# A two-layer hybrid mixer block: gate input evicted first, output weights loaded in order of use, last columns in two banks, and a new table of waiting times

## The chip, the cores and the metric

The kernel runs on one core of a Trainium2 chip. The metric is the time of one execution on the device in microseconds (us). A measurement is the median of several runs; beside them stands one execution recorded by the hardware profiler, from which all rows below come. The engines are TensorE (PE; its weight loads are PEld), VectorE (DVE), ScalarE (ACT), GpSimd (POOL) and SyncE (SP, which here only issues DMAs).

## The reference

Two layers act on 256 context and 256 latent tokens of width 1024. Each layer normalises its input, modulates it by a conditioning vector, runs four token mixers in parallel on it (multi-head latent attention, neighbourhood attention, Hyena long convolution, gated linear attention), gates each branch with SiLU, projects it to 1024, merges the four with sigmoid gates, applies one output projection, normalises and adds the residual:

```python
h = modulate(rms_norm(x, pre_g), shift, scale)
ys = [mla(h), na(h), hyena(h), gla(h)]                   # each (tokens, 512)
ys = [y * silu(in_proj(h, z)) for y, z in zip(ys, Z)]
merged = 0.25 * sum(sigmoid(in_proj(h, merge[i])) * (ys[i] @ w_branch[i]) for i in range(4))
x = x + gate * rms_norm(merged @ w_out, post_g)
```

Context tokens read only context; latents read both. Only the latent stream of the last layer is the output, so layer 1 computes the context only where latents need it. All inputs are float32.

## The kernel before

Tokens lie in four tiles of 128, as two pairs: pair 1 the context, pair 0 the latents; channels lie in chunks of 512. A float32 product is made of three matmuls of a rounded type (`mm3`): high part by high part, high by low, low by high, of which one takes 128 rows by up to 512 columns. A weight comes in a piece of 512 KB (`piece`, L426): SP loads it into one of three `raw` buffers, ACT rounds each half to `wh` (L439), DVE subtracts to get `wl` (L380). Both go into one of eight slots of the weight pool, or, for a piece marked spare, into tiles `w` of a larger pool. A `raw` buffer is free when both halves are subtracted; a slot is free when the last matmul has read it. PSUM is split into three pools: two banks for main products (pj, br, wo), four for helpers (pa, pc, lat, scores), two for transposes and small products (pt, glrp, ht, mt).

The order of PE's instructions is written out by the program, not found by a scheduler. A dozen generators (main thread, latents, attention, GLA, Hyena, filters, conditioning) yield; `drive` (L312) keeps a clock which each matmul and transpose advances by a modelled cost (`mm`, `tr`), and takes the first ready task by priority. A generator that yields `self.wait(name)` is ready again when the clock has moved on by the number in the table `WAIT` (one per layer, in us of PE work); the main thread (priority 5) fills what is between. So a larger number puts more main matmuls in front of a group. The other engines' instruction order, and which buffer a tile gets, are settled by a scheduler at build time from this program; every engine then executes its own list in order.

The change touches: `latents` (L897), which transposes the normalised low-rank rows of one token tile (lat into one PSUM bank, glrp, the gate's low-rank input, into another of a two-bank pool) and evicts them (cqT, ckvT, rotT, glrT); `project_out` (L1382), which loads the eight pieces of w_out, makes wo for each token tile in two halves of 512 columns, squares (ACT), multiplies by the gate (DVE), takes `rstd` (DVE, POOL), adds the residual (DVE) and stores; `merge_one` and `turn_merged` stand before it (br: branch product, gt: gated part on DVE, mt, mh, ml: the merged sum transposed and split).

Of the kernel before, what the change touches and what calls it, by code (L numbers as in the profile page):

```python
# [10 lines left out]
F32R = mybir.dt.float32r  # L11
U8 = mybir.dt.uint8
AF = mybir.ActivationFunctionType
# [112 lines left out]
def _layout(x, c, ctx, c_ctx, ada_w, ada_b, pre_g, post_g, w_in, mla_q_norm, mla_w_uq, mla_kv_norm, mla_w_ukv, na_rpb,  # L126
# [81 lines left out]
    "ada_at0": (3.68, 7.47),  # L208
    "ada_at1": (6.0, 11.0),
    "ada_at2": (15.0, 17.0),  # L210
    "ada_at3": (17.5, 19.5),
    "ada_sum": (1.34, 0),
    "ada_load": (7.75, 9.57),
    "ada_gap": (4.19, 8.22),
    "norm": (3.44, 4.0),
    "norm_turn": (6.66, 5.25),
    "norm_ab": (0.16, 0.69),
    "norm_step": (0.65, 0.52),
    "filt_in": (3.1, 4.0),
    "filt_sin1": (6.0, 15.54),  # L220
    "filt_sin2": (6.0, 4.8),
    "filt_w3": (4.0, 4.49),
    "filt_step": (0.48, 0.82),
    "filt_sum": (10.0, 11.8),
    "filt_norm": (7.2, 15.6),
    "filt_dft": (0.3, 0.5),
    "filt_out": (1.82, 4.04),
    "probs": (5.63, 6.08),
    "probs2": (7.2, 7.7),
    "probs_out": (1.36, 0.94),  # L230
    "values_out": (1.14, 5.3),
    "latent_in": (2.81, 1.5),
    "latents": (10.0, 11.79),
    "latents_out": (5.62, 0.49),
    "mla_keys": (1.6, 1.78),
    "mla_v": (0.32, 0),
    "mla_k": (0.8, 2.25),
    "mla_q": (0.15, 0),
    "mla_q_out": (1.7, 1.04),
    "na_in": (2.87, 0.97),  # L240
    "hy_turn": (1.49, 4.79),
    "hy_turn_step": (0.35, 0.5),
    "hy_turn_out": (0.5, 0.67),
    "hy_dft": (1.57, 2.98),
    "hy_product": (12.59, 11.95),
    "hy_mid": (0.35, 0.81),
    "hy_out_step": (0.72, 0),
    "hy_order": (6.38, 0.9),
    "hy_out": (1.3, 1.0),
    "gla_in": (2.65, 0.67),  # L250
    "gla_logit": (1.02, 0.1),
    "gla_decay": (7.1, 2.9),
    "gla_dir": (6.31, 4.0),
    "gla_norm": (14.0, 4.73),
    "gla_turn": (0.03, 0.45),
    "gla_out": (1.66, 1.98),
    "gla_keys": (6.49, 5.03),
    "gla_kT": (0.9, 1.07),
    "gla_at": (0.5, 0.5),
    "gla_scores": (5.09, 7.57),  # L260
    "gla_o": (2.0, 1.05),
    "merged": (4.6, 3.55),
    "merged_step": (0.48, 0),
    "merged_out": (0.82, 1.24),
    "norm_first": (3.27, 8.0),
}


class Task:
    def __init__(self, gen, prio, ready):  # L270
# [1325 lines left out]
```

## Time and profile before

| | |
|---|---|
| median of 3 runs | 1361.12 us (1359.09 to 1361.54) |
| profiled execution, its own time | 1358.52 us |
| its span, first to last instruction | 1356.7 us |
| mean granted PE clock | 0.993 |
| busy: PE, DVE, ACT, POOL | 1299.6, 889.4, 607.1, 318.3 us |
| DMA | 171.08 MB, mean 126 GB/s |

The busy time of an engine is the time in which it has an instruction running. In a timeline a row stands for one instruction or several alike in a row (xN); the bracket at its end is the idle time of the engine before it, and what ended it. Waits group these idle times by who ended them. A granted clock of 1.00 is TensorE's full speed of 2.4 GHz, 0.50 is 1.2 GHz; a stretch's number is the mean over it.

### The profile page before, as it was taken

Reading aid. Unit: us, or ns where it says so; the run is one execution under the profiler, and the core shown is the slowest. Engines: PE = TensorE matmul, PEld = TensorE weight load, DVE = VectorE, ACT = ScalarE, POOL = GpSimd, SP = SyncE. Lnnn points to the kernel's source line nnn. Section 1 sums busy time; section 2 is a strip of 40 time slices with the busy share of each in tenths; the row PEclk is TensorE's granted clock in tenths of the full one; section 3 lists DMA queues with packets and bytes.
Section 4 is the critical chain, followed back from the end, with each engine's and each line's share of the span. In section 5 each row is a group of like instructions: output and inputs, shape, how many; then the busy total and the mean of one; then the engine's idle time right before and its main releaser. Section 6 shows DMA issues by size and latency. Waiting matters only on the chain. (4 is left out here: it accounts for less than half of the span.)

```text
span 1356.7 us, 20161 instructions
## 1 busy us (share of the span) xinstructions
PE 1299.6 (96%) x7444; PEld 1023.7 (75%) x7444; DVE 889.4 (66%) x1660; ACT 607.1 (45%) x1282; POOL 318.3 (23%) x408
## 2 busy tenths in 40 slices
PE   5999999999999999999999999899999999999996
PEld 3877677777777776778767778787767899678875
DVE  5778666575143547676476597887579776768864
ACT  4655556233233332222344444575475456434552
POOL 2332213333030101124111123342123421121210
PEclk9999999999999999999999999999999999999999
DMA  9521222233243433324422352432135366434361
GB/s 350 214 93 40 93 70 77 94 110 109 94 155 124 145 120 108 124 94 139 142 77 80 114 192 85 138 106 99 48 115 158 115 211 212 156 101 153 118 208 63
DMA packets 55507, 171.08 MB, mean 126 GB/s; under 512 B 7470, under 2 KB 10128, under 8 KB 55408
## 3 DMA queue, kind: packets, MB, share of 16 engines
q1 hardware_dynamic: 49056, 153.31, 34.1%
q0 software_dynamic: 5440, 16.16, 3.8%
q8 instruction: 59, 0.97, 0.3%
q10 hardware_dynamic: 912, 0.31, 0.1%
q14 instruction: 40, 0.33, 0.1%
HBM read 163.45 MB, written 6.31 MB: 125 GB/s over the span
## 5 line engine op out<-in xcount | busy, mean ns | idle before, releaser
L380 DVE TENSOR_TENSOR wl<-raw,wh 128x512 fp32r<-128x512 f32 (+1 forms) x416 | 299.0, 740 | 191.2 <-ACT wh L439 186.3
L439 ACT CAST wh<-raw 128x512 fp32r<-128x512 f32 (+1 forms) x416 | 248.5, 617 | 285.1 <-DMA raw<-in_w_in 156.2
L390 PE MATMUL pc<-hh,wh 128*128 128x256 f32 (+1 forms) x688 | 239.8, 349 | 2.1 <-DVE kr L906 1.5
L390 PE MATMUL pc<-hh,wl 128*128 128x256 f32 (+1 forms) x688 | 229.8, 334 | 0.0
L390 PE MATMUL pc<-hl,wh 128*128 128x256 f32 (+1 forms) x688 | 229.3, 333 | 0.0
L390 PE MATMUL pj<-wh,hh 128*128 128x512 f32 x512 | 212.7, 415 | 1.5 <-ACT wh L439 0.8
L390 PE MATMUL pj<-wl,hh 128*128 128x512 f32 x512 | 200.6, 392 | 0.8 <-DVE wl L380 0.6
L390 PE MATMUL pj<-wh,hl 128*128 128x512 f32 x512 | 200.3, 391 | 0.0
L390 PEld LDWEIGHTS pc<-hh,wh 128*128 128x128 f32 x688 | 131.2, 191 | 25.6 <-issue 10.9
L390 PEld LDWEIGHTS pc<-hl,wh 128*128 128x128 f32 x688 | 131.2, 191 | 13.8 <-issue 2.4
L390 PEld LDWEIGHTS pc<-hh,wl 128*128 128x128 f32 x688 | 130.8, 190 | 13.3
L390 PEld LDWEIGHTS pj<-wh,hh 128*128 128x128 f32 x512 | 96.2, 188 | 32.3 <-issue 12.5
L390 PEld LDWEIGHTS pj<-wl,hh 128*128 128x128 f32 x512 | 96.4, 188 | 23.2 <-DVE wl L380 3.6
L390 PEld LDWEIGHTS pj<-wh,hl 128*128 128x128 f32 x512 | 96.1, 188 | 20.9
L380 POOL TENSOR_TENSOR gl<-y,gh 128x256 fp32r<-128x256 f32 (+1 forms) x44 | 36.6, 839 | 302.7 <-ACT gh L422 287.3
L826 ACT ACTIVATE p<-sc,mx 128x512 f32<-128x512 f32 (+1 forms) x96 | 59.0, 616 | 57.9 <-DVE mx L824 54.0
L390 PE MATMUL br<-wh,gh 128*128 128x512 f32 x192 | 77.2, 402 | 2.3 <-DVE gt L383 2.3
L390 PE MATMUL br<-wl,gh 128*128 128x512 f32 x192 | 75.1, 391 | 1.6 <-DVE wl L380 1.6
L390 PE MATMUL br<-wh,gl 128*128 128x512 f32 x192 | 74.9, 390 | 0.0
L1347 ACT ACTIVATE gt<-pj 128x512 f32<-128x512 f32 x48 | 28.6, 596 | 93.2 <-PE pj L390 93.0
L824 DVE TENSOR_REDUCE mx<-sc 128x1 f32<-128x512 f32 (+1 forms) x96 | 55.1, 591 | 11.5 <-PE sc L390 10.6
L377 POOL TENSOR_TENSOR merged<-merged,gt 128x512 f32<-128x512 f32 x24 | 33.1, 1385 | 83.8 <-DVE gt L383 83.8
(286 smaller groups left out, 2213.9 us busy)
## 6 DMA issues: line engine op xcount, KB each, us to landing
raw<-in_w_in SPq DMA_DIRECT2D x160, 512.0 KB, 3.6
adaw<-in_ada_w SPq DMA_DIRECT2D x36, 512.0 KB, 3.8
raw<-in_w_branch SPq DMA_DIRECT2D x32, 512.0 KB, 3.6
raw<-in_w_out SPq DMA_DIRECT2D x16, 512.0 KB, 4.4
adaw<-in_ada_w SPq DMA_DIRECT2D x24, 256.0 KB, 5.2
H<-filt POOLq DMA_DIRECT2D x16, 256.0 KB, 4.0
nab<-in_na_bias POOLq DMA_DIRECT2D x16, 256.0 KB, 3.0
raw<-in_w_in SPq DMA_DIRECT2D x8, 448.0 KB, 4.2
```

The lines of the kernel that those rows point to most:

```text
L377: eng.tensor_tensor(out=out, in0=a, in1=b, op=ALU.add)
L380: eng.tensor_tensor(out=out, in0=a, in1=b, op=ALU.subtract)
L390: self.nc.tensor.matmul(out, lhsT, rhs, start=start, stop=stop, skip_group_check=skip)
L439: nc.scalar.copy(hi, raw[:, sl])
L824: nc.vector.tensor_reduce(out=mx, in_=ps[h][:, :nk], axis=AX.X, op=ALU.max, negate=True)
L826: nc.scalar.activation(p[h][:, :nk], ps[h][:, :nk], AF.Exp, bias=mx, scale=1.0, accum_out=sm)
L1347: self.nc.scalar.activation(gates[s, t], ps, AF.Tanh, scale=0.5)
```

## The change

Four edits. In `latents`, the transpose of the gate input and its eviction glrT come ahead of the evictions of the latents. In `project_out`, the pieces of w_out are loaded as they are used (half 1's first two, half 0's first two, then the rest) instead of all of half 1 first; as before, half 1's pieces are spare tiles and half 0's take weight slots. For the last token tile of layer 1, half 0's 512 columns are made in two PSUM banks of 256 columns (`last_half`), with square, product and sum of each part after its matmuls; the end of the chain is spread over DVE, ACT and POOL. The modelled cost of a matmul gets 32 columns more, and 0.1 where the shape of the PE tile changes; the table of waits is scaled by about 1.06, and some entries are set anew.

```diff
-    "ada_gap": (4.19, 8.22),
-    "norm": (3.44, 4.0),
-    "norm_turn": (6.66, 5.25),
+    "ada_gap": (1.65, 8.71),
+    "norm": (4.8, 3.77),
+    "norm_turn": (5.59, 5.57),
...
-    "hy_mid": (0.35, 0.81),
+    "hy_mid": (0.37, 0),
...
-    "gla_turn": (0.03, 0.45),
+    "gla_turn": (1.89, 0.48),
...
-    "gla_kT": (0.9, 1.07),
-    "gla_at": (0.5, 0.5),
-    "gla_scores": (5.09, 7.57),
+    "gla_kT": (0.63, 1.13),
+    "gla_at": (0, 0.53),
+    "gla_scores": (4.1, 8.02),
...
-            cost = cols / 2400 if rhs.dtype == F32R else 4 * max(cols, 64) / 2400
+            cost = (cols + 32) / 2400 if rhs.dtype == F32R else 4 * max(cols, 64) / 2400
+        mode = (64 if lhsT.shape[0] <= 64 else 128, 32 if out.shape[0] <= 32 else 64 if out.shape[0] <= 64 else 128)
+        if mode != self.mode:
+            self.mode = mode
+            cost += 0.1
...
         parts = [(b, self.cqT[b], self.pp(l, "q_norm", b)) for b in range(2) if full] + [(2, self.ckvT, self.pp(l, "kv_norm"))]
+        pg = self.ps(self.pt, "glrp")
+        self.tr(pg[:96, 0:P], kr[:, 128:224])
+        nc.scalar.copy(self.glrT[:96, sl], pg[:96, 0:P])
         for b, dst, g in parts:
             nc.scalar.activation(dst[0][:, sl], pp[:, b, :], AF.Copy, scale=g)
...
-        pg = self.ps(self.pt, "glrp")
-        self.tr(pg[:96, 0:P], kr[:, 128:224])
-        nc.scalar.copy(self.glrT[:96, sl], pg[:96, 0:P])
...
-        ws = {half: self.rows([self.piece(d["w_out"][l, half, j], 2, 512, half == 1) for j in range(4)]) for half in (1, 0)}
+        order = [(half, j) for step in (0, 1) for half in (1, 0) for j in (2 * step, 2 * step + 1)]
+        got = {(half, j): self.piece(d["w_out"][l, half, j], 2, 512, half == 1) for half, j in order}
+        ws = {half: self.rows([got[half, j] for j in range(4)]) for half in (1, 0)}
...
+                        if last and half == 0:
+                            break
...
+                if last:
+                    yield from self.last_half(ps[0], [t[:, :, P : 2 * P] for t in mT[s]], ws[0], ss, gate[s][0], [o[half][:, 1, :] for half in (0, 1)], x)
+                    continue
...
+    def last_half(self, ps, m, w, ss, gate, y, x):
+        nc = self.nc
+        pair = [ps, self.ps(self.pmm, "wo")]
+        parts, junk = self.t(2, "lss"), self.T("junk")
+        sl = [slice(0, 256), slice(256, 512)]
+        sq = lambda g: nc.scalar.activation(junk[:, sl[g]], pair[g][:, 0:256], AF.Square, scale=D ** -0.5, accum_out=parts[:, g : g + 1])
+        times = lambda g: self.mul(nc.vector, y[0][:, sl[g]], pair[g][:, 0:256], gate[:, sl[g]])
+        for g in range(2):
+            for kt in range(KT):
+                self.mm3(pair[g][:, 0:256], [t[:, kt, :] for t in m], [t[:, sl[g]] for t in w(kt)], kt == 0, kt == KT - 1)
+                yield 0
+            sq(g)
+            if g == 0:
+                times(0)
+                self.add(nc.vector, ss[:, 0:1], ss[:, 1:2], parts[:, 0:1])
+        r, v = self.t(1, "rstd"), self.t(1, "ms")
+        self.ts(v, parts[:, 1:2], ss[:, 0:1], ALU.add, EPS, ALU.add)
+        nc.gpsimd.tensor_tensor(out=r, in0=v, in1=self.mhalf[:, :1], op=ALU.pow)
+        times(1)
+        nc.scalar.activation(y[0][:, sl[0]], y[0][:, sl[0]], AF.Copy, scale=r)
+        self.add(nc.gpsimd, y[0][:, sl[0]], y[0][:, sl[0]], x[0][:, sl[0]])
+        self.stt(y[1], y[1], r, x[1], ALU.mult, ALU.add)
+        nc.sync.dma_start(self.out[1][:, 512:1024], y[1])
+        nc.sync.dma_start(self.out[1][:, 0:256], y[0][:, sl[0]])
+        self.stt(y[0][:, sl[1]], y[0][:, sl[1]], r, x[0][:, sl[1]], ALU.mult, ALU.add)
+        nc.sync.dma_start(self.out[1][:, 256:512], y[0][:, sl[1]])
```

Line numbers of the rows below are those of each kernel, so the same call has another number after the change. First place: ACT, the latents of layer 0. lat_837, lat_852, lat_867 are the PSUM banks of the first three token tiles, glrp their gate inputs. Before, from the last copy of the second tile on:

```order
L935 COPY rotT_258<-lat_852 128x128
L934 ACTIVATE cqT_252<-lat_867,par_122 128x128
L934 ACTIVATE cqT_254<-lat_867,par_122 128x128
L934 ACTIVATE ckvT_256<-lat_867,par_122 128x128
L940 CAST glrT_259<-glrp_849 96x128
L940 CAST glrT_259<-glrp_864 96x128
...
L940 CAST glrT_259<-glrp_879 96x128
```

After, from the first gate input on:

```order
L943 CAST glrT_259<-glrp_842 96x128
L945 ACTIVATE cqT_252<-lat_837,par_122 128x128
L945 ACTIVATE cqT_254<-lat_837,par_122 128x128
L945 ACTIVATE ckvT_256<-lat_837,par_122 128x128
L946 COPY rotT_258<-lat_837 128x128
L945 ACTIVATE cqT_252<-lat_852,par_122 128x128
L945 ACTIVATE cqT_254<-lat_852,par_122 128x128
L943 CAST glrT_259<-glrp_857 96x128
L945 ACTIVATE ckvT_256<-lat_852,par_122 128x128
...
L943 CAST glrT_259<-glrp_872 96x128
```

The first gate input now stands ahead of all latents, the second behind two of the second tile's, and the third behind two of the third tile's.

Second place: the end of layer 0, where w_out's pieces come in. raw_7506 and raw_7516 are the first two pieces in either order; br_7356, br_7371 and br_7386 are branch products, gt what DVE makes of them. DVE before:

```order
L380 TENSOR_TENSOR w_7513<-raw_7506,w_7512 128x512
L383 SCALAR_TENSOR_TENSOR gt_6950<-gt_6950,br_7356 128x512
L380 TENSOR_TENSOR w_7519<-raw_7516,w_7518 128x512
L377 TENSOR_TENSOR merged_2506<-merged_2506,gt_6950 128x512
L380 TENSOR_TENSOR w_7523<-raw_7516,w_7522 128x512
L383 SCALAR_TENSOR_TENSOR gt_6991<-gt_6991,br_7371 128x512
L377 TENSOR_TENSOR merged_2506<-merged_2506,gt_6991 128x512
```

DVE after:

```order
L381 TENSOR_TENSOR w_7513<-raw_7506,w_7512 128x512
L381 TENSOR_TENSOR w_7519<-raw_7516,w_7518 128x512
L381 TENSOR_TENSOR w_7523<-raw_7516,w_7522 128x512
L384 SCALAR_TENSOR_TENSOR gt_6924<-gt_6924,br_7356 128x512
L378 TENSOR_TENSOR merged_2512<-merged_2512,gt_6924 128x512
L384 SCALAR_TENSOR_TENSOR gt_6977<-gt_6977,br_7371 128x512
L378 TENSOR_TENSOR merged_2512<-merged_2512,gt_6977 128x512
```

Both halves of the second piece now stand ahead of the first gt, which frees the PSUM bank of br_7356.

ACT at the same place, before, where raw_7526 and raw_7536 are the third and fourth pieces, and mh the split of the transposed merge:

```order
L439 CAST w_7528<-raw_7526 128x512
L439 CAST w_7532<-raw_7526 128x512
L439 CAST w_7538<-raw_7536 128x512
L439 CAST w_7542<-raw_7536 128x512
L1377 ACTIVATE mh_7420<-mt_7422 128x4x128
L1377 ACTIVATE mh_7420<-mt_7432 128x4x128
L439 CAST wh_7548<-raw_7546 128x512
```

ACT after, where raw_7526 and raw_7536 hold half 0's first pieces (cast to wh_7528 to wh_7542), raw_7546 and raw_7556 half 1's last:

```order
L447 CAST w_7548<-raw_7546 128x512
L447 CAST w_7552<-raw_7546 128x512
L1385 ACTIVATE mh_7420<-mt_7422 128x4x128
L447 CAST w_7558<-raw_7556 128x512
L1385 ACTIVATE mh_7420<-mt_7432 128x4x128
L447 CAST w_7562<-raw_7556 128x512
L447 CAST wh_7528<-raw_7526 128x512
L447 CAST wh_7532<-raw_7526 128x512
```

The third and fourth pieces by SP's order are cast behind the fifth and sixth, and the second mh stands behind a cast of the sixth.

Third place: PE at the start of layer 1. ht are the transposes of the second token pair (one row of four stands for each), pa products of the pair that was normalised first, f the filters, pc a product that takes its bank from the same pool as pa. Before:

```order
L390 MATMUL pa_8127<-wh_8102,hl_7883 128x224
...
L404 MATMUL ht_8264<-ident,xn_8180 128x128
...
L390 MATMUL f_2042_8314<-w3h_8134,a_1890_7695 128x512
...
L390 MATMUL pc_8339<-hh_7882,wh_8331 128x256
...
L404 MATMUL ht_8346<-ident,xn_8180 128x128
...
L390 MATMUL f_2063_8358<-w3h_8134,a_1890_7695 128x512
...
L390 MATMUL pc_8339<-hh_7882,wh_8331 128x256
...
L404 MATMUL ht_8371<-ident,xn_8181 128x128
```

After:

```order
L409 MATMUL ht_8252<-ident,xn_8168 128x128
...
L391 MATMUL pa_8127<-wh_8122,hh_7888 128x224
...
L409 MATMUL ht_8274<-ident,xn_8168 128x128
...
L391 MATMUL f_2044_8324<-w3h_8134,a_1888_7688 128x512
...
L409 MATMUL ht_8331<-ident,xn_8169 128x128
...
L391 MATMUL pc_8359<-hh_7888,wh_8351 128x256
...
L409 MATMUL ht_8366<-ident,xn_8169 128x128
```

The first transposes stand ahead of the last products pa, and three of four ahead of the first pc.

## Rows read from the trace of the kernel before

**Rows 1.** The profile page, its first line and the first row of busy time.

```profile
span 1356.7 us, 20161 instructions
...
PE 1299.6 (96%) x7444; PEld 1023.7 (75%) x7444; DVE 889.4 (66%) x1660; ACT 607.1 (45%) x1282; POOL 318.3 (23%) x408
```

**Rows 2.** Timeline, 72-75 us: start, duration, engine, line, operation, tiles, idle before.

```profile
72.42 0.47 ACT L940 CAST glrT<-glrp 96x128 fp32r<-96x128 f32 x2
...
72.77 0.32 PE L404 MATMUL glrp<-ident,kr 128*96 128x128 f32 x1 [1.89 <-ACT glrT L940]
...
74.32 0.63 PE L390 MATMUL pc<-hh,wh 128*128 128x512 f32 x1
```

**Rows 3.** Busy by stretch: length, PE, PEld, DVE, ACT, POOL, PEclk, DMA share, GB/s.

```profile
69.00:73.00 4.00, 2.12 (x18) 1.78 (x17) 4.00 (x8) 3.51 (x16) 1.81 (x2) 1.00 0.37 85
...
73.00:78.00 5.00, 5.00 (x19) 4.08 (x18) 3.13 (x10) 2.93 (x11) 0.00 (x0) 0.66 0.23 89
...
893.20:896.60 3.40, 3.40 (x17) 3.21 (x16) 1.89 (x7) 2.18 (x7) 1.00 (x3) 0.50 0.09 34
```

**Rows 4.** Waits of PE in 100 to 190 us: total, times, longest.

```profile
PE q L390 <- ACT wuq L422: 1.7, 2, 1.1
...
PE pt L404 <- DVE p L387: 1.3, 2, 0.7
```

**Rows 5.** Timeline of the first GLA, 262 to 295 us, PE and DVE.

```profile
262.91 0.73 PE L390 MATMUL atp<-qp,ktl 64*64 64x64 f32 x26
...
267.20 1.85 DVE L1314 COPY_PREDICATED at<-causal,atp 64x256 f32<-64x256 uint8 x4 [0.22 <-POOL at L1304]
...
290.67 1.29 DVE L380 TENSOR_TENSOR wl<-raw,wh 128x512 fp32r<-128x512 f32 x2 [3.44 <-ACT wh L439]
...
294.44 0.63 PE L404 MATMUL ktp<-ident,ktl 128*128 128x128 f32 x4 [1.46 <-DVE ut L383]
```

**Rows 6.** Timeline at the end of layer 0, DVE and PE.

```profile
786.70 1.76 DVE L380 TENSOR_TENSOR w<-raw,w 128x512 fp32r<-128x512 f32 x1
...
788.98 0.68 DVE L380 TENSOR_TENSOR w<-raw,w 128x512 fp32r<-128x512 f32 x1
...
789.11 0.50 PE L390 MATMUL br<-wh,gh 128*128 128x512 f32 x1 [1.94 <-DVE gt L383]
...
801.06 0.39 PE L390 MATMUL br<-wh,gl 128*128 128x512 f32 x1
```

**Rows 7.** The page, DMA issues: tiles, queue, count, KB each, median us to landing.

```profile
raw<-in_w_out SPq DMA_DIRECT2D x16, 512.0 KB, 4.4
```

**Rows 8.** Timeline of PE at the start of layer 1.

```profile
881.69 0.36 PE L390 MATMUL pc<-hh,wh 128*128 128x256 f32 x1 [1.51 <-DVE kr L906]
...
887.82 0.36 PE L390 MATMUL pa<-wh,hl 128*128 128x192 f32 x1 [0.61 <-DVE hl L380]
...
892.52 0.36 PE L390 MATMUL pa<-wh,hl 128*128 128x192 f32 x1 [1.04 <-DVE hl L380]
```

**Rows 9.** Waits of PE, whole span: total, times, longest.

```profile
PE pj L390 <- DVE wl L380: 0.6, 3, 0.2
```

**Rows 10.** Timeline: 256-column matmuls at 883 us, then the end of the program.

```profile
883.49 0.28 PE L390 MATMUL pc<-hl,wh 128*128 128x256 f32 x1
...
883.61 0.28 PE L390 MATMUL pc<-hh,wl 128*128 128x256 f32 x1
...
1346.67 0.39 PE L390 MATMUL wo<-wl,mh 128*128 128x512 f32 x1
...
1346.90 0.39 PE L390 MATMUL wo<-wh,ml 128*128 128x512 f32 x1
...
1347.32 0.60 ACT L1409 ACTIVATE junk<-wo 128x512 f32<-128x512 f32 x1 [4.75 <-PE wo L390]
...
1348.04 0.69 DVE L374 TENSOR_TENSOR o<-wo,gate 128x512 f32<-128x512 f32 x1 [4.75 <-ACT junk L1409]
...
1348.93 0.56 POOL L411 TENSOR_TENSOR rstd<-ms,mhalf 128x1 f32<-128x1 f32 x1 [10.30 <-DVE ms L387]
```

More of the change, by code (lines that the diff above doesn't have):

```diff
@@ L207 @@
 WAIT = {
[L208 to L213, printed above, removed]
-    "ada_gap": (4.19, 8.22),
-    "norm": (3.44, 4.0),
-    "norm_turn": (6.66, 5.25),
[L217 to L241, printed above, removed]
@@ L259 @@
-    "gla_at": (0.5, 0.5),
-    "gla_scores": (5.09, 7.57),
[L261 to L265, printed above, removed]
+    "ada_at0": (3.9, 7.92),
+    "ada_at1": (6.36, 9.93),
+    "ada_at2": (15.9, 18.02),
+    "ada_at3": (18.55, 20.67),
+    "ada_sum": (0.71, 0.0),
+    "ada_load": (8.21, 10.14),
+    "ada_gap": (1.65, 8.71),
+    "norm": (4.8, 3.77),
+    "norm_turn": (5.59, 5.57),
+    "norm_ab": (0.17, 0.73),
@@ new lines @@
+    "norm_step": (0.69, 0.26),
+    "filt_in": (3.17, 3.48),
+    "filt_sin1": (6.36, 11.83),
+    "filt_sin2": (6.94, 5.09),
+    "filt_w3": (4.24, 3.41),
+    "filt_step": (0.51, 0.87),
+    "filt_sum": (10.6, 11.74),
+    "filt_norm": (7.63, 16.54),
+    "filt_dft": (0.32, 0.53),
+    "filt_out": (1.93, 4.28),
+    "probs": (5.97, 6.44),
+    "probs2": (7.63, 8.16),
+    "probs_out": (1.44, 1.0),
+    "values_out": (1.21, 5.62),
+    "latent_in": (2.98, 1.59),
+    "latents": (10.6, 12.72),
@@ new lines @@
+    "latents_out": (5.96, 0.52),
+    "mla_keys": (1.7, 1.89),
+    "mla_v": (0.67, 0.0),
+    "mla_k": (0.85, 2.39),
+    "mla_q": (0.16, 0.0),
+    "mla_q_out": (1.8, 1.1),
+    "na_in": (4.17, 1.7),
+    "hy_turn": (1.58, 5.08),
+    "hy_turn_step": (0.35, 0.53),
+    "hy_turn_out": (0.53, 0.71),
+    "hy_dft": (1.66, 3.16),
+    "hy_product": (13.35, 12.67),
+    "hy_mid": (0.37, 0),
+    "hy_out_step": (0.76, 0.0),
+    "hy_order": (6.76, 0.95),
+    "hy_out": (1.38, 1.06),
+    "gla_in": (2.81, 0.71),
@@ L266 @@
+    "gla_logit": (1.08, 0.11),
+    "gla_decay": (7.53, 3.07),
+    "gla_dir": (6.69, 4.24),
+    "gla_norm": (14.84, 5.01),
+    "gla_turn": (1.89, 0.48),
+    "gla_out": (1.76, 2.1),
+    "gla_keys": (6.88, 5.98),
+    "gla_kT": (0.63, 1.13),
+    "gla_at": (0, 0.53),
+    "gla_scores": (4.1, 8.02),
+    "gla_o": (2.12, 1.11),
+    "merged": (4.88, 3.76),
+    "merged_step": (0.51, 0.0),
+    "merged_out": (0.87, 1.31),
+    "norm_first": (3.47, 8.48),
 }
@@ L298, in __init__ @@
         self.clock = 0.0
+        self.mode = (128, 128)
         self.l = 0
@@ L404, in tr @@
         self.nc.tensor.transpose(out, in_, self.ident)
+        if self.mode != (128, 128):
+            self.mode = (128, 128)
+            self.clock += 0.1
         self.clock += 0.107
@@ L1394, in project_out @@
                     ps = {half: self.ps(self.pmm, "wo") for half in (1, 0)}
+                last = i == 1 and l == DEPTH - 1 and s == streams[-1]
                 for step in (0, 1) if i == 0 else ((0, 1),):
```

14 lines of the change are left out of this document (removed).

## The prediction

> **What bounds the kernel now.** I read the page first, then the waits of PE, then the timeline where those waits sit, and the clock by stretch. The page says that PE decides: it is busy for 1299.6 of 1356.7 us, and no other engine is above 66% [rows 1]. So the time can move in three ways only: the number and length of matmuls, the idle time of PE, and the clock that PE is granted. The change leaves the matmuls as they are but for one place (24 of 512 columns become 48 of 256). What it can win or lose is therefore waits, some 57 us of idle PE in all (1356.7 less 1299.6), scattered in pieces of 0.3 to 2 us, and the half-rate stretches that follow some of them. A new table of waiting times shifts hundreds of PE groups by a few matmuls; only where a group stood next to a wait does that matter. I went through these places in order of time, comparing the order of the engines before and after.
>
> **The change, part by part.** Terms are microseconds on the profiled execution, which took 1358.5 us by its own time (span 1356.7 and 1.8 around it); that is 2.6 below the median of the three runs, 1361.1, so the sum is carried over to the median as a difference.
>
> *Gate input first, layer 0.* The transpose into glrp at 72.77 has waited 1.89 us for ACT's glrT at 72.42 [rows 2]: the two PSUM buffers of that pool come free only when ACT has got through the latents of three tiles. In 69 to 73 PE works 2.12 of 4 us, and then in 73 to 78 the granted clock is 0.66 on average although PE is busy throughout [rows 3]: 0.34 of 5 us, 1.7 us, is lost at the lower level (the matmul at 74.32 takes 0.63 us [rows 2]; it comes down to 1.2 GHz). After the change glrT of the first tile leaves ACT before any latent, and that of the second after seven copies instead of twelve. ACT is 3.51 of 4 us busy there [rows 3], so the transposes of the fourth tile still find a copy to wait for; I leave 0.8 of the 1.89 and take 1.1 plus the whole 1.7: **-2.8**. From both sides: the wait can move whole to the next latent's buffer (0), or go with the clock fall (-3.6).
>
> *Start and MLA of layer 0.* In 100 to 190 us PE waits 1.7 us for the query weights and 1.3 for p [rows 4]. After the change three groups that wait there have three to six main matmuls more ahead of them; the query weights stand where they stood. I take back most of the 1.3: **-1.2**, with 0 to -3 for the other waits of this stage; the first 70 us are dealt out anew (their first matmuls, transposes and conditioning weights change places), which I put at nothing, 1.5 either way.
>
> *First GLA of layer 0.* The masked scores of the second pair of chunks end on PE at 263.64 and their four copies on DVE at 269.05, 5.4 us later [rows 5]. Before, PE came back for them well after that. The new table (gla_at 0 instead of 0.5, gla_scores 4.10 instead of 5.09) has PE back after 15 main matmuls and one conditioning group, some 4.2 us: a new wait of 1.2. The transposes at 294.44 already wait 1.46, since DVE sat 3.44 us for the weight behind 290.67 and the state chain stood behind it [rows 5]. After the change the same two weight halves stand inside the chain, and their transfer waits for a conditioning group that is now only 6 us of PE ahead of it; 0.6 longer. **+1.8**, from 0 (copies find DVE free) to +4 (the third and fourth pair wait too).
>
> *Order of w_out, end of layer 0.* The matmul at 789.11 waits 1.94 us for gt on DVE, which stood behind one subtraction of 1.76 us [rows 6]. In the new order two more subtractions of w_out, 7518's and 7522's, stand ahead of this gt: 0.60 each at the pace of the 0.68 instruction at 788.98, so +1.2. Further: the third and fourth transfers are now the first pieces of half 0. These are not spare tiles; they take the slots of the branch weights, which PE reads until the last matmul of that branch's pair at 801.06 [rows 6]. So two of the three raw buffers hold pieces that can't be cast, and the next three pieces go through one: each needs 4.4 us to land [rows 7] and then two casts and two subtractions, about 0.65 each, before the next. By ACT's order the second cast of the transposed merge (mh) now stands behind such a cast, and by DVE's order ml and the gt that frees the next branch's PSUM stand behind its subtraction. Counting from the end of 7522's subtraction near 790, 4.4 + 2.6 + 4.4 + 0.6 puts that cast at 802 and the gt near 804, where PE wants its buffer 1.2 later than before, near 803: +1.2; and the first output matmul, which needs the following gt, +1.0. **+3.4** in all, from +1.2 (only the first) to +8 (subtractions at 1.76 and a clock fall behind the waits). In layer 1 no matmul waits for a w_out weight, and mh and ml keep their place behind the same number of casts: 0.
>
> *Start of layer 1.* PE waits 1.51 at 881.69, 0.61 at 887.82, 1.04 at 892.52 [rows 8], and from 893.2 the clock is 0.50 for 3.4 us [rows 3], which costs 1.7. The new order puts three of the four transposes of the second token pair ahead of the first products pc, and DVE and ACT take their modulation up to ten places earlier, so hl, by the count of instructions that no longer stand ahead of it, is ready 1.2 to 2.3 us sooner. The wait at 881.69 is for kr, which stays behind the same weight and now behind one more modulation: it stays. Of the 1.65 of hl I take 1.3, and the 1.7 of the clock: **-3.0**; -0.9 if the clock falls all the same and kr comes later, -4.2 if the waits between go too.
>
> *Rest of layer 1.* In the hyena stage three or four subtractions of weights stand one product further back on DVE, just where PE now waits 0.6 in three pieces for wl [rows 9]: **+0.5**, -1 to +1.5.
>
> *Last 512 columns.* Matmuls of 256 columns start 0.12 us apart (883.49, 883.61), those of 512 columns 0.23 (1346.67, 1346.90) [rows 10]: 48 by 0.118 less 24 by 0.23 is +0.2 with rounding. Behind them, ACT's square covers 256 columns, about 0.2 less than 0.60, and the last matmul itself is 0.1 shorter; above all ms no longer stands behind the 0.6 of DVE's product at 1348.04 [rows 10]. That makes -0.9. What follows rstd stays: instead of two instructions on DVE (twice 0.7, as the product at 1348.04) it is a scale on ACT and then an addition on POOL, after which the last transfer is issued, also about 1.4; I count nothing for the halved transfer. **-0.6**, from -1.4 to +0.3.
> The Trainium skill, TensorEngine Tiling (Array Packing), section Instruction Overhead, speaks against this edit: each matmul carries some 60 cycles of its own. By that, 24 more matmuls at 2.4 GHz would cost 0.6 us instead of 0.2, an estimate from that page, and this term would be -0.2. The trace doesn't agree: two starts of 0.118 against one of 0.23 leave next to nothing for the second instruction.
>
> Sum: -2.8 - 1.2 + 1.8 + 3.4 - 3.0 + 0.5 - 0.6 = **-1.9**: 1356.6 for the profiled execution, 1359.2 at the median.
>
> **The rivals.** *A: the loads stay hidden.* If DVE and ACT reach the moved gt, mh and copies in time, because transfers land in less than 4.4 us or an engine works off its queue while PE is on main matmuls, the +1.8 and +3.4 vanish: -7.1, 1354.0. For it: the view of PE's waits has one only between 780 and 815 us, the 1.94 at 789.11, so there is slack; against it: engines take their instructions in order, and the order is fixed. *B, slower: w_out blocks the end of layer 0.* The two subtractions run at 1.76, as the one before them does, instead of 0.60: +2.3. The chain of single-buffer loads is 1 us later for it, and four waits close together bring the clock down once, 1.7. That is +5.0 on the sum, +3.1 in all: 1364.2. It decides from 4.6 us of loss there beyond the 3.4, for only then is the sum slower by more than a measurement tells apart. *C: waits move only.* Without the clock gains of 1.7 at 73 and 893 us (the level falls after other waits) and with the loss in the GLA halved: -1.9 + 3.4 - 0.9 = +0.6, 1361.7. *D: the table doesn't act*, its shifts all landing between waits; then w_out, latents and tail alone are left, -2.8 + 3.4 - 0.6 = 0.0, 1361.1.
>
> **How the numbers follow.** Forecast 0.45, A 0.20, B 0.20, C and D together 0.15. A measurement of this kernel tells about 0.2%, 2.7 us, from no change. The forecast at -1.9 with its own range of 1356 to 1362.5 gives 0.20 faster, 0.23 no change, 0.02 slower; A all faster; B 0.19 slower; C and D 0.11 no change, 0.02 each side. Together, with rounding, 0.42, 0.35 and 0.23. The half-widths of the terms (1.8, 2.3, 2, 3.4, 1.7, 1.3, 0.9), taken as independent, make 5.5, and the medians of three runs some 1.2 more; so 1351.5 to 1366.
>
> **What would show it.** In the profile after: PE's glrp wait of 1.89 under 1 and a clock of 1.00 in 73 to 78; go waiting 1 us or more for DVE's copies near 265; br's wait for gt at 789 growing to 3, and two new waits before the first output matmul; the waits on hl near 887 and 892 gone and no half-rate stretch behind them; in the last 10 us ms ahead of DVE's product. The prediction is wrong where br waits no longer than before (A), where a clock fall near 790 to 805 appears (B), or where the half-rate stretches stay (C).

## The result, and the profile after

The changed kernel takes 1369.41 us (median of 5 runs, 1365.16 to 1371.32); the kernel before, beside it, 1359.09 (5 runs). The ratio is 1.0064, 95% interval 1.0046 to 1.0081. The forecast was 1359.2 with a range to 1366.0: it is outside, on the slow side. The profiled execution took 1371.32 us, 12.8 more than that of before (the medians are 10.3 apart).

The page of the changed kernel, its first line and its first row of busy time, answers to [rows 1]:

```profile
span 1369.5 us, 20212 instructions
...
PE 1308.9 (96%) x7468; PEld 1031.1 (75%) x7468; DVE 889.3 (65%) x1662; ACT 605.3 (44%) x1285; POOL 325.3 (24%) x409
```

PE is busy 9.3 us longer with the same work (24 matmuls more, of half the size), so most of the loss is not idle time as such. It is time at the lower clock: by the granted clock, four stretches lose some 10.2 us (450 to 456 us at 0.72, 795 to 803 and 877 to 885 at 0.57, 1334 to 1339 at 0.66), where before three lose 5.1 (73 to 78, 869 to 873, 893.2 to 896.6), and the start adds some 4. To see where, I laid the traces side by side: for each matmul, its start after less its start before, less what the work ahead of it had changed. Read in order of time, the lag grows and shrinks as follows; the sum is the 12.8. Between 250 and 790 us groups have changed places, and how the sum of those four rows, +5.0, is split is an estimate; at the other borders the same work lies ahead of the matmul in both kernels.

| stretch (us, after) | lag gained | forecast |
|---|---|---|
| start, to 70 | +5.3 | 0 (±1.5) |
| gate input, 70 to 84 | -2.6 | -2.8 |
| MLA and branches, to 250 | -1.7 | -1.2 |
| first GLA, 250 to 311 | +3.1 | +1.8 |
| up to the hyena's input, to 424 | +0.4 | not listed |
| hyena's input, 424 to 457 | +5.0 | not listed |
| hyena, NA, to 790 | -3.5 | not listed |
| end of layer 0, 790 to 803 | +4.1 | +3.4 |
| start of layer 1, to 946 | +0.8 | -3.0 |
| rest of layer 1 | +1.0 | +0.5 |
| last 512 columns, to the end | +0.9 | -0.6 |

**Start.** The first 448-column products of the changed kernel, by the timeline of PE:

```profile
32.81 0.57 PE L391 MATMUL pa<-wl,hh 128*128 128x448 f32 x1
33.18 0.57 PE L391 MATMUL pa<-wh,hl 128*128 128x448 f32 x1
...
38.43 0.36 PE L391 MATMUL pa<-wl,hh 128*128 128x448 f32 x1
38.63 0.37 PE L391 MATMUL pa<-wh,hl 128*128 128x448 f32 x1
```

and the same view of the kernel before:

```profile
28.06 0.37 PE L390 MATMUL pa<-wl,hh 128*128 128x448 f32 x1
28.26 0.37 PE L390 MATMUL pa<-wh,hl 128*128 128x448 f32 x1
```

Starts lie 0.37 apart at 33 us after, 0.20 at 28 us before. 448 columns in 0.37 us are 1.2 GHz: PE was still at the lower level when these products came, and the first of these rows stands 4.75 us later. No wait in the list of PE's waits tells of it, and the view by stretch prints a clock of 1.00 there, because the trace's records of the granted clock begin only at 38 us in this kernel; only the spacing of equal matmuls tells.

**Gate input.** The waits of PE from 70 to 80 us, and two stretches of busy time [rows 2, 3]:

```profile
PE glrp L409 <- ACT glrT L943: 0.9, 1, 0.9
```

```profile
73.00:78.00 5.00, 4.15 (x29) 3.48 (x28) 3.63 (x8) 3.30 (x13) 2.82 (x3) 1.00 0.40 106
77.60:82.60 5.00, 4.95 (x19) 3.45 (x20) 4.75 (x15) 5.00 (x18) 0.00 (x0) 1.00 0.40 110
```

The 1.89 became 0.9. The wait now ends at 77.65, so the second row is the stretch behind it: the clock stays 1.00. This term came as forecast.

**First GLA.** PE's waits that answer to [rows 5], from the timeline (start, duration, ..., in brackets the idle time before it and its cause):

```profile
271.98 0.46 PE L391 MATMUL go<-gla_v,at 128*128 128x128 f32 x2 [0.19 <-DVE at L1322]
273.23 1.80 PE L391 MATMUL go<-gla_v,at 128*128 128x128 f32 x14 [0.79 <-POOL st L388]
293.69 0.63 PE L409 MATMUL ktp<-ident,ktl 128*128 128x128 f32 x4 [1.38 <-DVE ut L384]
301.40 0.64 PE L391 MATMUL ada<-adaw,sv 128*32 128x256 f32 x8 [1.56 <-issue]
```

The go is there with about 1 us in two waits, ktp is as it was, and the conditioning group ada waits where nothing waited; its wait is ended by "issue", that is by nothing that the profile shows.

**Hyena's input, the term I did not have.** Timeline of PE:

```profile
446.11 0.47 PE L391 MATMUL pc<-hh,wh 128*128 128x512 f32 x1 [1.07 <-DVE cv L384]
...
450.36 0.61 PE L391 MATMUL adat<-par,rows 128*128 128x2 f32 x4 [1.92 <-DVE rows L378]
450.82 0.63 PE L391 MATMUL pc<-hh,wh 128*128 128x512 f32 x1
...
454.55 0.40 PE L391 MATMUL pc<-hh,wh 128*128 128x512 f32 x1
```

and the stretch with its clock:

```profile
450.00:456.00 6.00, 5.64 (x20) 4.56 (x21) 2.49 (x6) 1.15 (x2) 1.28 (x1) 0.72 0.51 178
```

Before, PE has no wait from 430 to 450 us. Now adat, the second half of a conditioning group, comes back before DVE has written its rows, since ada_gap of layer 0 went from 4.19 to 1.65 (the run gap_restored below shows that this entry is the cause). Two waits, 3.0 us together, and behind them nine products at 0.43 instead of 0.23.

**End of layer 0** [rows 6]. Timelines of DVE, POOL and PE:

```profile
789.95 1.78 DVE L381 TENSOR_TENSOR wl<-raw,wh 128x512 fp32r<-128x512 f32 x1
791.66 1.78 DVE L381 TENSOR_TENSOR w<-raw,w 128x512 fp32r<-128x512 f32 x1
793.36 1.74 DVE L381 TENSOR_TENSOR w<-raw,w 128x512 fp32r<-128x512 f32 x1
795.03 0.68 DVE L381 TENSOR_TENSOR w<-raw,w 128x512 fp32r<-128x512 f32 x1
795.63 0.67 DVE L384 SCALAR_TENSOR_TENSOR gt<-gt,br 128x512 f32<-128x512 f32 x1
```

```profile
787.74 6.82 POOL L375 TENSOR_TENSOR gate<-gate,pg 128x512 f32<-128x512 f32 x4
```

```profile
796.36 0.80 PE L391 MATMUL br<-wh,gh 128*128 128x512 f32 x1 [3.29 <-DVE gt L384]
796.95 0.63 PE L391 MATMUL br<-wl,gh 128*128 128x512 f32 x1
```

DVE is never idle between the subtractions and gt; three of w_out's stand directly ahead of it. The two that run beside POOL's products for the gate take 1.78 and 1.74 us, the third, behind them, 0.68. The wait grows from 1.94 to 3.29, and the clock falls. The two further waits of my chain of raw buffers are not there.

**Start of layer 1** [rows 8]. Timeline of PE:

```profile
893.58 0.36 PE L391 MATMUL pc<-hh,wh 128*128 128x256 f32 x1 [1.07 <-DVE kr L916]
...
913.18 0.38 PE L391 MATMUL pc<-hh,wh 128*128 128x256 f32 x1 [2.28 <-DVE zg L384]
...
944.15 0.66 PE L409 MATMUL pt<-ident,p 128*128 128x128 f32 x4 [1.51 <-DVE pt L847]
```

Both waits on hl are gone, as forecast, and with them the fall at 893; that stretch wins some 5. Then PE waits 4.4 us for zg and pt (with one wait of 0.56 for zg that is not shown) where before it waited 1.5 in all from 895 to 950. And the fall ahead of it has moved and grown; first the row of before, then that of after:

```profile
869.00:873.00 4.00, 4.00 (x24) 4.00 (x23) 3.68 (x8) 1.50 (x3) 1.41 (x3) 0.57 0.95 259
877.00:885.00 8.00, 7.00 (x35) 7.00 (x36) 6.39 (x13) 2.86 (x7) 3.42 (x5) 0.57 0.93 289
```

**Tail** [rows 10]. DVE, then SP, then POOL:

```profile
1360.07 0.21 DVE L388 TENSOR_SCALAR ms<-lss,pss 128x1 f32<-128x1 f32 x1 [2.39 <-ACT junk L1445]
1360.20 0.41 DVE L375 TENSOR_TENSOR o<-wo,gate 128x256 f32<-128x256 f32 x1
```

```profile
1362.98 0.43 SPq L1463 DMA_DIRECT2D out<-o  x1
```

```profile
1361.55 0.75 POOL L378 TENSOR_TENSOR o<-o,x 128x256 f32<-128x256 f32 x1 [0.62 <-ACT o L1459]
```

ms is ahead of the product. From the start of the last matmul (1359.25) to the end of the last issue it takes 4.16 us, before 4.41 (1346.90 to 1351.31). But the span does not end with the stores. From the start of the last matmul to its end it is 10.3 us, before 9.85. In both kernels it ends 7.2 us behind POOL's last instruction: before, that was rstd, done at 1349.49; now it is the addition, done at 1362.30. So the end comes 0.45 later, and not 0.25 earlier.

### The profile page after: what moved, and what is told of

Same layout as the page of the kernel before. It is cut to its first block, busy times and chain, and to the rows that moved or that the text cites. A ratio compares the mean times of both kernels' runs of the same rounds, so it can differ in the third digit from the quotient of the medians.

```text
span 1369.5 us, 20212 instructions
## 1 busy us (share of the span) xinstructions
PE 1308.9 (96%) x7468; PEld 1031.1 (75%) x7468; DVE 889.3 (65%) x1662; ACT 605.3 (44%) x1285; POOL 325.3 (24%) x409
## 5 line engine op out<-in xcount | busy, mean ns | idle before, releaser
L381 DVE TENSOR_TENSOR wl<-raw,wh 128x512 fp32r<-128x512 f32 (+1 forms) x416 | 302.6, 750 | 190.2 <-ACT wh L447 185.8
```

The costliest lines, as they stand in the source:

```text
L381: eng.tensor_tensor(out=out, in0=a, in1=b, op=ALU.subtract)
```

## The experiments

Theory after the first look: the planner's clock (the modelled costs by which `drive` counts time, not the clock that PE is granted) and the table of waits cost it, the code edits do little. Rival: w_out's order costs the end of layer 0. Times are medians, each beside the kernel before on the same chip; brackets are the 95% interval of the ratio.

### Code edits against table

edits_only is the changed kernel with the old cost lines and the old table; table_only is the kernel before with only these two new.

```diff
 # edits_only, against the changed kernel
-cost = (cols + 32) / 2400 ...        # and the two mode costs
+cost = cols / 2400 ...
-WAIT = {new}
+WAIT = {old}
```

> The kernel before with the three code edits (gate input first, w_out in order of use, last 512 columns in two banks), and with the old table of waits and the old clock. Theory 1 (the 10 us come from the new table and clock): no slower than before, 1354 to 1358 us; glrp's wait of 1.9 gone, br's wait near 789 as before (2 us). Theory 2 (the edits cost, w_out's order above all, as the prediction had it): 1361 to 1364, with br waiting 3 us or more.

> The kernel before with the new table and clock and none of the code edits. Theory 1: 1368 to 1374 us, with the half-rate start to 38 us, the waits near 446 to 451 and the 3.4 us wait of br in it. Theory 2: 1362 to 1366.

edits_only: 1360.45 to 1360.44, ratio 1.0002 [0.9988, 1.0016]. table_only: 1369.33, 1.0065 [1.0044, 1.0087]. The whole loss is the planner's clock with its table; the three edits together are worth nothing that can be measured. In edits_only PE's instructions stand in the order of the kernel before up to the last 48 matmuls.

The parts of the code edits by themselves, each put into the kernel before; latents_last is the gate input and the last 512 columns together:

> The kernel before with the gate input's edit alone. Prediction's step: glrp's wait of 1.9 and the half-rate stretch behind it go, -1.5 to -3 us, 1357.5 to 1359. Rival (the time won comes back as a half-rate stretch later): 1360 to 1361, with the clock full through 78 us all the same.

> The kernel before with the new order of w_out's pieces alone. Prediction's step (raw buffers held, mh behind a cast, gt late): +2 to +3.4 us, 1362.5 to 1364, with new waits near 802 and 808. Rival (DVE's order is another one without the table, loads hidden): 1360 to 1361, br's wait at 2 us.

> The kernel before with the last 512 columns in two banks alone. Prediction's step: +0.2 us of matmuls, 0.9 off the chain behind them, -0.6 in all: 1359 to 1360, so no change that this many runs can tell; in the trace the end of the program 0.5 to 1.4 us nearer to the last matmul of 512 or 256 columns. Rival (the addition on POOL after a scale on ACT is slower than DVE's second product): 0 to +0.5 us.

> The kernel before with the gate input's edit and the last 512 columns in two banks, w_out in the old order, old table and clock: what the runs so far point to as the fastest. If the two gains add (2.6 and 0.6): 1356.5 to 1357.5, faster than before by 0.2 to 0.3%. Rival (the time won at 73 us comes back as a half-rate stretch near 790 and 866): 1359 to 1360.

latents_only 0.9981 [0.9969, 0.9994], wout_only 1.0000 [0.9983, 1.0017], last_only 1.0015 [1.0001, 1.0029], latents_last 1.0013 [0.9998, 1.0029]. Only the gate input wins, 2.3 us of 1360.02, and narrowly; edits_only and latents_last, which hold the same edit, do not, so the win is not certain. Its trace shows the won time being given back. By stretch:

```profile
73.00:78.00 5.00, 5.00 (x20) 3.45 (x19) 4.77 (x13) 4.78 (x14) 0.00 (x0) 1.00 0.14 57
786.00:790.00 4.00, 4.00 (x12) 3.12 (x11) 3.88 (x7) 2.02 (x4) 0.00 (x0) 0.57 0.72 217
864.00:872.00 8.00, 6.30 (x31) 6.30 (x32) 6.87 (x13) 2.19 (x5) 3.39 (x4) 0.57 0.94 295
```

and in the kernel before:

```profile
786.00:790.00 4.00, 2.06 (x10) 1.37 (x9) 4.00 (x5) 0.66 (x2) 1.91 (x2) 1.00 0.43 138
864.00:872.00 8.00, 5.49 (x35) 5.31 (x36) 7.68 (x15) 2.88 (x8) 3.91 (x5) 0.83 0.88 266
```

The fall at 74 is gone (clock 1.00), but one has come behind the wait for gt (0.57 in 786 to 790), where the kernel before keeps 1.00 through a wait of the same length, and the one near 870 has grown. The same two losses, 1.4 and 1.2 us by the lag, stand in edits_only and latents_last, and in neither wout_only nor last_only: they go with this edit, and take back the 2.0 to 2.5 us that it wins in 70 to 84 us of these three traces.

The last 512 columns cost time. The 0.25 between the last matmul and the last issue is saved (in last_only too, 1346.49 to 1350.65), but 48 starts 0.12 apart cost 5.76 where 24 took 5.46, and the end of the span stands 0.45 further from the last matmul's start: 10.3 us in every kept trace with this edit, 9.85 in the four without it (before, latents_only, wout_only, table_only). In all of them it ends 7.2 us behind POOL's last instruction. That the addition on POOL is the reason is read from these traces; no run moved it to another engine.

### Which order at the end of layer 0

wout_undone is the changed kernel with the old order of w_out.

```diff
-order = [(half, j) for step in (0, 1) for half in (1, 0) ...]
...
+ws = {half: self.rows([... for j in range(4)]) for half in (1, 0)}
```

> The changed kernel with w_out loaded in the old order, half 1 first. The prediction's step (the order of the pieces puts two subtractions ahead of gt and holds two raw buffers): br's wait falls from 3.4 to 2 us or less and the half-rate stretch behind it goes, 1364 to 1366 us. Rival (the order of DVE there comes from the table, since two subtractions stand ahead of gt in this kernel too): br waits 3 us or more, 1368 to 1371.

1367.5, ratio 1.0049 [1.003, 1.0067]. PE's waits from 785 to 806 in it, and busy by stretch:

```profile
PE br L391 <- DVE gt L384: 3.3, 1, 3.3
```

```profile
794.00:798.00 4.00, 3.51 (x9) 2.79 (x10) 3.96 (x7) 1.62 (x3) 0.00 (x0) 0.57 0.66 204
798.00:802.00 4.00, 4.00 (x20) 3.27 (x19) 2.41 (x5) 0.00 (x0) 0.00 (x0) 1.00 0.70 250
```

The wait of 3.3 stays with w_out in its old order, and table_only has it too (3.3); wout_only, with the new order alone, does not (two waits of 3.0 together, the longer 2.0). So the table puts the subtractions ahead of gt. One entry is enough: in gap_restored, below, which keeps the new order of w_out and takes back ada_gap of layer 0 alone, one subtraction stands directly ahead of gt and the wait is 2.0 again. What the new order of w_out adds is at most what follows: the clock is back at 1.00 by 798 here, and at 803 in the changed kernel, 1.6 us by the lag, in one profile each. The ratios, 1.0049 and 1.0064, are not told apart: their intervals overlap.

### The entries that stand at the new waits

gap_restored puts ada_gap of layer 0 back (4.19 times 1.06), start_restored norm_turn and ada_sum of layer 0, which bring back the old order of the first 350 PE instructions.

```diff
-"ada_gap": (1.65, 8.71),    "norm_turn": (5.59, 5.57),   "ada_sum": (0.71, 0.0),
+"ada_gap": (4.44, 8.71),    "norm_turn": (7.06, 5.57),   "ada_sum": (1.42, 0.0),   # each in its kernel
```

> The changed kernel with one entry of the table taken back: ada_gap of layer 0 at 4.44 (the old 4.19 times 1.06) instead of 1.65. Theory 1 (the conditioning product is read back too soon, so adat waits for DVE, and the clock falls behind it): the waits at 446 and 451 and the half-rate stretch behind them go, and the 1.6 at 301: 1362 to 1365 us. Rival (these waits come from DVE's work on the Hyena input, whoever asks for it): 1368 to 1370.

> The changed kernel with two entries of layer 0 taken back: ada_sum 1.42 instead of 0.71 and norm_turn 7.06 instead of 5.59, which gives PE the old order in its first 350 rows. Theory (PE's early order leaves it idle in pieces, and the full clock is granted only at 38 us instead of 16 to 31): full clock by 31 us, 4 us less at 40 us, 1364 to 1366 us. Rival (the clock's start is chance from run to run): full clock anywhere from 16 to 38, 1368 to 1370.

gap_restored: 1371.11, 1.0082 [1.005, 1.0114]. PE has no wait from 437 to 456 and the clock is 1.00 in 450 to 456, so the short gap is the cause of the 5 us there:

```profile
450.00:456.00 6.00, 6.00 (x33) 4.38 (x32) 3.02 (x6) 1.82 (x3) 1.36 (x2) 1.00 0.38 107
```

But two others take their place, one row of PE's waits in 280 to 300 and one in 480 to 496:

```profile
PE adat L391 <- DVE ut L384: 4.1, 1, 4.1
```

```profile
PE hyt L409 <- DVE cv L384: 2.7, 1, 2.7
```

The short gap was what hid the first GLA's late DVE and the hyena's transposes (scaled, below, has the same entry and the same two waits). start_restored: 1369.0, 1.0055 [1.0035, 1.0076]. In its profile the first products still run at 0.37 to 31 us, but full rate follows from 33, and the lag from 40 to 72 us is 1.7 instead of 5.3. That is more than chance: at the same matmul near 72 us, the five traces with the changed kernel's first order of PE lag by 4.1 to 5.3, the ten with the old one by -0.9 to 3.3. The start of layer 1 then wins 0.5 instead of 5.5 by 905 us: the waits on hl are back (1.4 in two), with a clock of 0.52 in 893 to 900. The likely reason is norm_turn, which is read with layer 0's value also for the first norm of layer 1; it was not run apart from ada_sum. One entry serves several places, and can mend one at the cost of another.

### What is wrong with the planner's clock and the table?

Two theories: the planner's new clock counts small matmuls dearer than 1.06 times (256 columns 1.125, 128 columns 1.25), so waits scaled by 1.06 run out too early; or else its cost of a mode switch (a change of the PE tile's shape) shifts the groups. scaled is the changed kernel with all old entries times 1.06, none of the 22 re-set ones (two more, 0.02 and 0.22 off the factor, go back with them); scaled_no_mode drops the mode cost from it; retunes_old_clock has the old planner's clock with the 22 re-set entries (over 1.06).

> The changed kernel (code edits and new clock) with every entry of the table at the old value times 1.06, so without the 22 entries set anew. Theory 1a (the entries set anew cost the time): 1359 to 1362 us, with the old start, br's wait near 2 us and no waits of adat behind DVE in the Hyena input. Rival 1b (the clock's fixed parts and the scale move the groups into waits): 1366 to 1370.

> The scaled kernel (code edits, old table times 1.06) with the 32 columns more for each matmul, but without the 0.1 for a change of the tile's shape. Theory (the waits of the GLA run out too soon since its many small matmuls now advance the clock; the 0.1 falls nearly all into the GLA): the 9.5 us lost between 249 and 300 shrink to 3 or less, the 7 us at the start of layer 1 stay, 1374 to 1377. Rival (the 32 columns alone do it): 1380 to 1383.

> Code edits and the old clock; of the table only the 22 entries set anew, divided by 1.06. Theory (the new clock costs, the entries set anew win part of it back, and are of no use without it): 1362 to 1368, slower than with the old entries. Rival (the entries set anew are better by themselves): below 1358.

scaled 1382.26, 1.0157 [1.0134, 1.0181]; scaled_no_mode 1381.54, 1.0165 [1.0147, 1.0182]; retunes_old_clock 1380.63 (three runs, 1372.54 to 1381.35), 1.0139 [1.0109, 1.017]; no profile of it is read here. The mode cost is not it. Of the new clock's 1.6% the re-set entries win back 0.9; without the new clock the same entries cost 1.4. They suit the order that the new clock makes, and not the old one. PE's waits in scaled, whole span:

```profile
PE adat L391 <- DVE ut L384: 6.1, 2, 5.1
...
PE hyt L409 <- DVE cv L384: 3.5, 1, 3.5
```

The test of the first theory: own_scaled gives each entry the growth of the matmuls that stood behind its own wait, layer1_own does it for layer 1 of the changed kernel only.

```diff
 # own_scaled, against scaled; some of its entries
-"gla_dir": (6.69, 4.24),  "gla_keys": (6.88, 5.33),  "probs": (5.97, 6.44),
+"gla_dir": (8.67, 5.17),  "gla_keys": (8.87, 6.51),  "probs": (6.51, 7.16),
```

> The changed kernel with its new clock, whose table has none of the 22 re-set entries; beyond the start of layer 0 (whose entries stay times 1.06) each entry is the old one times the growth that the new clock itself gives to the matmuls that stood behind that wait in the old order (gla_dir of layer 0 1.375, gla_keys 1.37, probs 1.16 to 1.18, hy_turn of layer 1 1.125, ada_gap of layer 0 1.09). Theory (one factor of 1.06 was too small for stretches of small matmuls, so their waits ran out early): the losses of the scaled table at 249-300, 475-492 and 904-941 us go, and the time falls from 1382 to 1358-1364 (ratio 0.998 to 1.004). Rival (the one factor is not what hurts; the new clock places work worse whatever the table, or one value for a wait that stands in unlike stretches can't follow it): 1370 or more, with the waits of the scaled table still there.

> The changed kernel, table and all, with the layer-1 half of the table alone set to the old entry times the growth that the new clock gives to that wait's own matmuls (hy_turn 1.125, pieces of norm 1.09 to 1.14, gla_dir 1.29). Theory (the re-set entries of layer 1, and its short waits at one factor, made the new waits of 2.3, .7 and 1.5 us at 904-945): these three shrink below 1 us together with no new ones, and the kernel comes out 3 to 6 us below the changed one, ratio to the kernel before 1.002 to 1.004. Rival (they come from layer-0 entries that are still in use when layer 1 begins, such as norm_turn): they stay, ratio 1.006 or more.

own_scaled 1397.46, 1.029 [1.027, 1.031]; layer1_own 1376.26, 1.0126 [1.0109, 1.0143]. The theory falls as it was put, for it asked for 0.998 to 1.004: waits that follow the clock more closely make it worse. (That one entry can't suit all the places where it is read, the other half of the rival, was not tested by itself.) In layer1_own PE waits 1.1 instead of 2.8 for zg and 0.5 instead of 1.5 for pt, as expected; but its scores wait 6.4 us for q, whose matmuls were done by 926.3. The timelines of DVE and ACT show why:

```profile
927.12 0.69 DVE L381 TENSOR_TENSOR wl<-raw,wh 128x512 fp32r<-128x512 f32 x1 [2.88 <-ACT wh L447]
...
929.77 3.35 DVE L771 RECIPROCAL rn<-rn 128x512 f32<-128x512 f32 x1
933.16 0.42 DVE L375 TENSOR_TENSOR q<-q,qtab 128x256 f32<-128x256 f32 x1
```

```profile
932.52 1.14 ACT L447 CAST wh<-raw 128x512 fp32r<-128x512 f32 x2 [3.89 <-DMA raw<-in_w_in]
933.62 0.41 ACT L430 CAST q<-q 128x256 fp32r<-128x256 f32 x1
```

The first step behind PE's q is DVE's product with a table (933.16). It stands on DVE behind a subtraction that waited 2.88 us for a weight cast, and a reciprocal of 3.35. ACT's copy starts when that product is done; a weight cast ahead of it, which waited 3.89 for its transfer though DMA is busy only 0.26 of 920 to 940, ends at the same moment. Either engine's list alone would have held q. The planner's wait says nothing of what stands ahead on another engine's queue.

So a simpler theory: the old table is fitted to the one order that it gives, and any shift costs, whatever the planner's clock. All three runs have the code edits; jitter_one and jitter_two keep the old planner's clock and multiply each old entry by 0.94 or 1.06 at random; longer_old_clock multiplies all by 1.06.

> The three code edits under the old clock, with the old table whose entries are each multiplied by 0.94 or 1.06, drawn at random (first draw; ada_gap of layer 0 4.44, norm_turn 7.06, gla_keys 6.10). Theory (the old table is fitted to the very order it gives, and any shift of six per cent in its entries costs, with no new clock needed): ratio to the kernel before 1.005 to 1.015, with PE waits of 2 us or more in new places. Rival (the old table sits in a flat place, and it is the new clock with its unequal growth that misplaces work): ratio 0.998 to 1.003.

> The same with a second draw (ada_gap of layer 0 4.44, norm_turn 6.26, gla_dir 5.93). Theory of the fitted table: 1.005 to 1.015, but with the new waits in other places than in the first draw. Rival: 0.998 to 1.003.

> The three code edits under the old clock, with every entry times 1.06: all groups come back six per cent later by the same clock. Theory of the fitted table: 1.005 to 1.015. Rival (unequal growth is what costs, an equal one doesn't): 0.998 to 1.003. A third possibility: longer waits are safer and it is slightly faster, 0.997.

jitter_one 1382.0, 1.0159 [1.0138, 1.018]; jitter_two 1391.45, 1.0218 [1.0187, 1.0249]; longer_old_clock 1394.77, 1.0253 [1.0232, 1.0273]. All three lose as much as the new clock with its scaled table or more. PE's longest totals in jitter_two, but for the first wait of the program:

```profile
PE ktp L404 <- DVE ut L383: 6.0, 3, 2.2
PE pt L404 <- ACT pt L841: 5.4, 6, 2.8
```

and in longer_old_clock:

```profile
PE pc L390 <- DVE zg L383: 4.9, 3, 2.9
```

The places differ, the order of size doesn't. This is what a fitted table would show, and it rules out the rival, a table in a flat place: on the old table's own clock, six per cent in its entries cost 1.6 to 2.5%, 2.5 to 4 times what the changed kernel loses. Shifts smaller than six per cent were not tried. Whether a table fitted as long to the new clock would beat the old pair stays open; none was run.

## Why the prediction was wrong

**The step that failed** is the one that framed the sum: "only where a group stood next to a wait does that matter", and "I went through these places", those with a wait before. Two of the largest losses stand where before there was no wait, or none that the list of waits shows: the hyena's input (+5.0) and the start (+5.3). An order shift matters wherever a group stands less than the shift from its producer, whether or not it waits now; how many such places there are was not counted. The jitters put a price on them: +22 to +31 us for entries moved by six per cent. My terms, taken as independent and of both signs, averaged that out to -1.9. (The half-widths make 5.4, and with 1.2 more a lower end of 1352.5 instead of 1351.5; the upper end, on which the miss turns, is right.)

**Start**, "which I put at nothing, 1.5 either way": +5.3. Idle time was not the cost but the level at which the first products run. start_restored puts the order of the first 350 instructions at 3.6 of it; the rest is within what traces of one order differ by.

**Gate input**, -2.8: right, -2.6 here, and -2.0 in latents_only. That the clock falls elsewhere for it was half of rival C, and is what the three traces with this edit and the old table show: 2.6 given back at 786 to 792 and near 870. The term had no place for it. The 1.7 for the clock was not certain either: in last_only the same transpose waits 2.34 us and the clock behind it stays 1.00.

**MLA**, -1.2: right, -1.7. PE waits 0.5 for pt and 2.2 for the query weights there; those for p are gone [rows 4].

**First GLA**, +1.8: right in kind, +3.1. go waits 1.0 instead of the 1.2 forecast and ktp no longer than before; ada's 1.6, which I did not see, makes up for it (in gap_restored it is gone, with other waits in its place).

**w_out**, +3.4: the size is near (+4.1), the mechanism wrong, so that the nearness is luck. The wait grew by 1.35 where I had 1.2 for "two more subtractions"; but it is the table that puts them there (wout_undone, table_only), and not all take 0.60: of the three ahead of gt, two take 1.78 and 1.74, as rival B had it. The chain of raw buffers did not occur. In its place the clock fell, 2.7 of the 4.1: rival B's other half, behind one wait instead of four.

**Start of layer 1**, -3.0: the half that I looked at came (hl gone, -5 there), and the next 50 us took it back, +5, by new waits on zg and pt. They stand behind the piece of the order that I compared. The longer fall ahead of it, at 877 to 885, was in no term; with the old table it comes with the gate input's edit.

**Rest of layer 1**, +0.5: +1.0. The waits of pj for wl are 0.6 in three, as before [rows 9], so the mechanism did not act; the loss is at the last output matmuls, where the clock is 0.66 in 1334 to 1339.

**Last 512 columns**, -0.6: +0.9. ms is ahead as said, and 0.25 is saved up to the last issue, less than the 0.9 forecast: what follows rstd is not "also about 1.4". From the end of rstd to the end of the last issue it takes 2.48 us (1360.93 to 1363.41), before 1.82 (1349.49 to 1351.31). DVE's two sums take 1.61 instead of 1.42, and two issues stand behind the second of them, since SP takes its three in order; the addition on POOL was done 0.7 before the last. But the term's main gap is another: it ended with the last issue. The span ends 7.2 us behind POOL's last instruction, and the edit gave POOL a later one.

The matmuls are +0.3, for +0.2. By the Trainium skill, TensorEngine Tiling (Array Packing), section Instruction Overhead, 24 more matmuls would cost 0.6, an estimate from that page. The rows lie between: starts at 0.120 for 256 columns and 0.2275 for 512 make 0.0125 us of fixed time each, half of the page's 60 cycles. The measurement, 0.3, decides.

Rival C had the right direction, that gains at one place return as waits at another, but sized it from the old waits. The runs show waits of 1.9 (hyena's input), 4.1 (gap_restored) and 6.4 us (layer1_own) where before there was none or one of 0.3: the rows of before gave no bound for them.

## What to carry to other kernels

A table of waits that has been fitted to an order is a local best: treat any edit that moves the whole order (a planner's clock, a cost, a factor) as a loss until it is fitted again (here 0.6 to 2.9%), and test it apart from the code edits. In judging a new order, look at each group whose distance to its producer shrinks, not at the groups that wait now, and count on each engine's queue what stands ahead of the producer. Then add PE's clock: waits of 1 to 3 us can cost about as much again in the stretch behind them. And ask which engine's last instruction the end of the program follows before moving work to it.

## What the runs showed of the hardware

The level of PE's clock at the start depends on the order of the first instructions and on the run: before, 448-column products are 0.20 apart at 28 us; in edits_only, with the same order, the first are 0.37 apart at 29.8 and turn to full rate at 30.57; in the changed kernel, and in the four other traces with its first order, they are 0.37 apart until about 34.

A fall can come or not behind the same wait. Behind gt's wait of 2.0 the clock is 1.00 in the kernel before, wout_only, last_only and gap_restored, and below it in latents_only, latents_last and edits_only, the three with the gate input's edit and the old table:

```profile
786.00:790.00 4.00, 3.04 (x10) 2.42 (x11) 3.97 (x7) 0.00 (x0) 0.00 (x0) 0.79 0.74 257
```

The subtractions of weights on DVE (128x512) take 0.62 to 1.84 us for the same shape in the changed kernel and in the one before. What the long ones share is POOL: in all 18 traces that were read, every one that overlaps no instruction of POOL takes 0.70 us or less (362 of 496 in the kernel before), and every longer one overlaps one. No run moved POOL's work to test it.

The span ends 7.24 or 7.25 us behind the end of POOL's last instruction in all 18 traces, with that instruction 2.60 or 3.05 us behind the start of the last matmul; the last issue of a store stands 5.4 or 6.1 ahead of the end.
